# Matmuls whose moving tile and output are walked in short runs from several segments

## Chip, cores and metric

The kernel runs on one core of a Trainium2 chip. The metric is the time of one execution on the device, in microseconds (us). Two timed executions of the kernel before took 899.40 and 896.99 us, a median of 898.19. A further execution was recorded by the hardware profiler; all profile lines come from it.

## The reference

One block of an encoder: 512 tokens of width 1024. Three token mixers work on a normalised copy of the input, each has a gate, the gated sum goes through an output projection and is added to the input, and a feed-forward part with a short convolution follows.

```python
h = rms_norm(x, mix_norm_g[l])
proj = h @ w_in[l]                                  # q, k, v, o, gates of all mixers, merge_pre
...
gates = sigmoid(merge_pre + b_merge_gate[l])
g_ml, g_na, g_xa = split(gates, 3)
merged = g_ml * (y_ml @ w_br_ml[l]) + g_na * (y_na @ w_br_na[l]) + g_xa * (y_xa @ w_br_xa[l])
x = x + merged @ w_out[l]
a, u = split(rms_norm(x, ffn_norm_g[l]) @ w_up, 2)  # 2816 features each
x = x + (gelu(dwconv3(a, w_conv, b_conv)) * u) @ w_down
```

All of it is float32.

## The kernel before

Activations lie with features on the 128 partitions and tokens along the free dimension, so a projection gives one tile of 128 output features by 512 tokens at a time. A tile is one bank of the accumulation memory (PSUM), 512 float32 for each partition.

A float32 product is made out of three matmuls in a rounded float32 type (`F32R`): weights and activations are both split in a high and a low part, and `mm3` (L204) adds high times high (L205), high weight times low activation (L206) and low weight times high activation (L207) into the same output. The stationary operand is a block of 128 x 128 weights; the moving operand is 512 tokens of one block of 128 input features.

`proj` (L348) makes one tile: it takes the split weights of a block from `weights(key)`, a bank from a pool, and calls `mm3` for the 8 blocks of input features (`KT`, 1024 / 128), 24 matmuls in all. The keys name the projection: `mlk`, `xaq`, `o`, `memk`, `naq`, `nak` for the mixers' inputs, `g` for the merge gates (3 mixers by 8 tiles, L995), `out` for the output projection (8 tiles, L1039), and `ua` and `uu` for the two halves of the feed-forward up projection (22 tiles each, L1178 to L1203). Feature tile 0 of `ua` and `uu` is written out with `mm3` directly (L1176 to L1187), so 21 tiles of each go through `proj`. Tiles of the down projection (`dn`) and of the branches (`br`) call `mm3` without `proj`.

Weights come from memory in blocks by DMA from SyncE's queue, three blocks ahead, and are split by ScalarE (L187) and VectorE (L188) one block ahead. The order of the work is the order of the program: TensorE takes its matmuls one after another, and the mixers' smaller steps (generators that `step` advances) are put in between the projections. A result tile is read by VectorE or ScalarE as a whole: the gates at L996, the output at L1040, `ua` in `conv` at L391, `uu` at L1202.

In the neighbourhood attention, the scores (L747 and L748) take their moving tile as 8 rows of 32 columns, 64 columns apart, `KS[e][:, :, CW[b]:CW[b] + 32]`, and write 256 contiguous columns; the values (L785) take 256 contiguous columns. The transposes at L766 are plain float32 matmuls with 128 columns.

Of the kernel before, what the change touches and what calls it, by code (L numbers as in the profile page):

```python
# [20 lines left out]
KT = D // P  # L21
# [83 lines left out]
def hybrid_block(ctx, tc, xg, xT, memT, wflat, vecs, gbias, nabias, outa, outb):  # L105
# [27 lines left out]
    def mmps():  # L133
        return mmp.tile([P, 512], F32, tag="mm", name=nm("mm"))
# [58 lines left out]
    def weights(key):  # L193

        i, _, n = BINDEX[key]
        while st["raw"] <= min(i + RAW_AHEAD, len(BLOCKS) - 1):
            emit_raw(st["raw"])
            st["raw"] += 1
        while st["split"] <= min(i + SPLIT_AHEAD, len(BLOCKS) - 1):
            emit_split(st["split"])  # L200
            st["split"] += 1
        return split.pop(i)

    def mm3(ps, lh, ll, rh, rl, start, stop):  # L204
        PE.matmul(ps, lh, rh, start=start, stop=False)  # L205
        PE.matmul(ps, lh, rl, start=False, stop=False)  # L206
        st["mm"] = PE.matmul(ps, ll, rh, start=False, stop=stop).ins  # L207
# [137 lines left out]

    norm = []

    def proj(key, XHs, XLs, n=S, bank=None, at={}):  # L348
        ws = weights(key)
        ps = (bank or mmps)()  # L350
        for k in range(KT):
            mm3(ps[:, :n], ws[k][0], ws[k][1], XHs[k], XLs[k], k == 0, k == KT - 1)
            if k in at:
                at[k]()
        return ps
# [3 lines left out]
    for k in range(KT):  # L359
        if k % 2 == 0:  # L360
            ws = weights(("mlq", k // 2))
# [4 lines left out]
        for f in range(4):  # L366
            fs = slice(f * P, (f + 1) * P)
            if k == 0 and f == 0:
# [3 lines left out]
                for i, (w, x, j) in enumerate(((wh, XH, 0), (wl, XH, 0), (wh, XH, 1), (wl, XH, 1), (wh, XL, 0), (wh, XL, 1))):  # L372
                    PE.matmul(ps_q[0][:, hs[j]], w[:, fs], x[0][:, hs[j]], start=i == 0, stop=False)
                continue
            mm3(ps_q[f], wh[:, fs], wl[:, fs], XH[k], XL[k], k == 0, k == KT - 1)

    ps_k = [proj(("mlk", 0), XH, XL, bank=atps, at={1: lambda: norm.append(rstd_cols(acc, S, "x")),
                                                    7: lambda: norm.append(rstd_row(norm[0], S, "x"))})]
    rc, rb = norm
    ps_k.append(proj(("mlk", 1), XH, XL, bank=atps))  # L380
    SY.dma_start(gbf, gbias.partition_broadcast(P))
    rcc = cp.tile([P, NT], F32, name="rcc")
# [4 lines left out]
    def conv(ps, rbt, w, b, i, n):  # L387

        pad = pads[npad[0] % 2]
        npad[0] += 1  # L390
        V.tensor_tensor(pad[:, 1:513], ps, rbt, op=ALU.mult)  # L391
        t1 = scr()
        A.activation(t1, pad[:, 0:512], AF.Identity, scale=vcol(w, i), bias=vcol(b, i))  # L393
        V.scalar_tensor_tensor(t1, pad[:, 1:513], vcol(w, n + i), t1, op0=ALU.mult, op1=ALU.add)  # L394
        V.scalar_tensor_tensor(t1, pad[:, 2:514], vcol(w, 2 * n + i), t1, op0=ALU.mult, op1=ALU.add)  # L395
        return t1
# [9 lines left out]
    for f in range(4):  # L406
        ps = ps_k[f] if f < 2 else proj(("mlk", f), XH, XL)
        silu2(kT, slice(f * S, (f + 1) * S), conv(ps, rb, "mlw", "mlb", 4 + f, 8))
# [26 lines left out]
    for c in range(4):  # L435
        n = 272 if c == 0 else 256
        pss = [(mmps if c % 2 else atps)() for _ in range(NT)]
        for h in range(2):
            ws = weights(("tm", c, h))
            for t in range(NT):  # L440
                tsl = slice(t * P, (t + 1) * P)
                for k in range(4):
                    kk = 4 * h + k
                    ps = pss[t][:, :n]
                    mm3(ps, XH[kk][:, tsl], XL[kk][:, tsl], ws[k][0], ws[k][1], kk == 0, kk == KT - 1)
        for t in range(NT):
            ps = pss[t]
# [479 lines left out]
    for f in range(4):  # L927
        ps = proj(("xaq", f), XH, XL)
# [3 lines left out]
    for f in range(4):  # L932
        ps = proj(("o", f), XH, XL)
# [15 lines left out]
    for f in range(4):  # L949
        ps = proj(("memk", f), MH, ML, M)  # L950
# [3 lines left out]
    for i in range(4):  # L954
        ws = weights(("memv", i))
# [10 lines left out]
    for f in range(4):  # L966
        ps = proj(("naq", f), XH, XL)
# [3 lines left out]
    for f in range(4):  # L971
        ps = proj(("nak", f), XH, XL)
# [12 lines left out]
    for br in range(3):  # L985
# [18 lines left out]
        for fp in range(4):  # L1004
# [5 lines left out]
            ws = weights(("br", br, fp))  # L1010
            for i in range(2):
                f = 2 * fp + i
                ps = mmps()
# [22 lines left out]
    for f in range(KT):  # L1036
        xr = scr()
        SY.dma_start(xr, xT[f])
        ps = proj(("out", f), GH, GL)  # L1039
# [130 lines left out]
    for hh in range(2):  # L1170
# [3 lines left out]
        for j in range(HF):  # L1174
            f = HF * hh + j
            if f == 0:  # L1176
# [7 lines left out]
                k = KT - 1  # L1184
# [8 lines left out]
            c = conv(pa, rb2, "ffw", "ffb", f, FT)  # L1193
# [10 lines left out]
        for f in range(KT if hh == 0 else LF - 1):  # L1204
            ws = weights(("dn", hh, f, 0)) + weights(("dn", hh, f, 1))
            ps = mmps()
# [123 lines left out]
```

## Time and profile before

| what | value |
|---|---|
| median of two timed runs | 898.19 us |
| profiled execution | 899.74 us |
| its span, first to last instruction | 898.0 us |
| mean granted TensorE clock | 1.000 |
| VectorE, ScalarE, GpSimd busy | 579.5, 451.6, 165.2 us |
| matmuls of 128 x 512 at L205, high weights from `wh`, tokens from a unit tile, into an `mm` bank | 1022, mean 397 ns |
| weight loads at L205 | 1076, mean 188 ns |
| DMA, mean over the span | 111 GB/s |

A matmul's duration runs from its start to a modelled end, and the next matmul begins before that; the distance from one start to the next tells what a matmul costs in a row of them. Group lines give line, engine, operation, output and inputs, shape, count, then busy time, mean duration in ns, and the idle time of the engine before them with what ended it. Lines of a timeline give start and length in us, then the same names.

### The profile page before, as it was taken

Reading aid. Unit: us, or ns where it says so; the run is one execution under the profiler, and the core shown is the slowest. Engines: PE = TensorE matmul, PEld = TensorE weight load, DVE = VectorE, ACT = ScalarE, POOL = GpSimd, SP = SyncE. Lnnn points to the kernel's source line nnn. Section 1 sums busy time; section 2 is a strip of 40 time slices with the busy share of each in tenths; the row PEclk is TensorE's granted clock in tenths of the full one; section 3 lists DMA queues with packets and bytes.
Section 4 is the critical chain, followed back from the end, with each engine's and each line's share of the span. In section 5 each row is a group of like instructions: output and inputs, shape, how many; then the busy total and the mean of one; then the engine's idle time right before and its main releaser. Section 6 shows DMA issues by size and latency. Waiting matters only on the chain.

```text
span 898.0 us, 12449 instructions
## 1 busy us (share of the span) xinstructions
PE 890.3 (99%) x4446; PEld 747.2 (83%) x4446; DVE 579.5 (65%) x1154; ACT 451.6 (50%) x950; POOL 165.2 (18%) x236
## 2 busy tenths in 40 slices
PE   9999999999999999999999999999999999999997
PEld 7899878988888888888888888888888888888887
DVE  6794586756566757998766547766733476667433
ACT  6463455645545647899634435444422344444442
POOL 4201231102070660420000211111100011111010
PEclk9999999999999999999999999999999999999999
DMA  7223643422242453443323422222132322222412
GB/s 250 95 91 127 191 143 105 165 95 94 84 128 71 118 141 106 140 131 118 118 94 106 141 105 93 96 95 93 65 100 95 116 95 94 94 94 88 132 39 94
DMA packets 39293, 99.69 MB, mean 111 GB/s; under 512 B 5688, under 2 KB 13624, under 8 KB 39232
## 3 DMA queue, kind: packets, MB, share of 16 engines
q1 hardware_dynamic: 31584, 92.39, 29.8%
q0 software_dynamic: 7360, 6.32, 3.1%
q8 instruction: 35, 0.57, 0.3%
q14 instruction: 26, 0.21, 0.1%
q10 hardware_dynamic: 288, 0.20, 0.1%
HBM read 94.67 MB, written 4.21 MB: 110 GB/s over the span
## 4 chain that ended last, share of the span: by engine, by line
PE 95%; DMA 1%; ACT 1%; DVE 1%; issue 1%; POOL 0%; SPq 0%; POOLq 0%; DVEq 0%
PE mm L206 28%; PE mm L205 28%; PE mm L207 28%; PE at L205 2%; PE at L206 2%; PE at L207 2%; PE at L785 1%; PE at L640 1%; PE at L766 1%; PE at L608 1%; PE at L642 1%; DMA R<-rd 1%; DMA wr<-wflat 0%; PE at L623 0%; PE at L873 0%
## 5 line engine op out<-in xcount | busy, mean ns | idle before, releaser
L205 PE MATMUL mm<-u,wh 128*128 128x512 f32 (+1 forms) x1076 | 420.6, 391 | 0.5 <-ACT wh L187 0.5
L206 PE MATMUL mm<-u,wh 128*128 128x512 f32 (+1 forms) x1076 | 418.8, 389 | 0.0
L207 PE MATMUL mm<-u,wl 128*128 128x512 f32 (+1 forms) x1076 | 417.4, 388 | 0.0
L187 ACT ACTIVATE wh<-wr 128x512 fp32r<-128x512 f32 (+1 forms) x298 | 185.2, 624 | 264.7 <-PE mm L206 219.3
L188 DVE TENSOR_TENSOR wl<-wr,wh 128x512 fp32r<-128x512 f32 (+3 forms) x299 | 212.6, 712 | 113.2 <-ACT wh L187 108.5
L205 PEld LDWEIGHTS mm<-u,wh 128*128 128x128 f32 x1076 | 202.6, 188 | 43.6 <-ACT wh L187 0.8
L207 PEld LDWEIGHTS mm<-u,wl 128*128 128x128 f32 x1076 | 202.6, 188 | 43.5
L206 PEld LDWEIGHTS mm<-u,wh 128*128 128x128 f32 x1076 | 202.7, 188 | 42.1 <-DVE u L212 0.3
L1199 POOL TENSOR_TENSOR s<-s,rb 128x512 f32<-128x512 f32 x22 | 36.9, 1676 | 258.2 <-DVE s L1198 250.1
L473 POOL DMA_DIRECT2D u<-nav_d x128 | 62.3, 516 | 75.2 <-PE at L785 34.5
L211 ACT ACTIVATE u<-s 128x512 fp32r<-128x512 f32 x26 | 16.4, 631 | 53.5 <-DVE s L1202 53.2
L1047 POOL TENSOR_TENSOR acc<-acc,s 128x512 f32<-128x512 f32 x7 | 9.1, 1302 | 128.2 <-ACT s L1046 128.2
L1202 DVE TENSOR_TENSOR s<-mm,s 128x512 f32<-128x512 f32 x22 | 15.2, 689 | 21.4 <-POOL s L1199 21.4
L393 ACT ACTIVATE s<-pad,vec 128x512 f32<-128x512 f32 x30 | 24.4, 813 | 8.6 <-DVE pad L391 8.6
L212 DVE SCALAR_TENSOR_TENSOR u<-s,u 128x512 fp32r<-128x512 f32 x26 | 18.0, 692 | 14.3 <-ACT u L211 14.1
L394 DVE SCALAR_TENSOR_TENSOR s<-pad,vec,s 128x512 f32<-128x512 f32 x30 | 22.5, 751 | 6.1 <-ACT s L393 6.1
L205 PE MATMUL mm<-wh,u 128*128 128x256 f32 (+1 forms) x80 | 24.6, 307 | 0.0
L206 PE MATMUL mm<-wl,u 128*128 128x256 f32 (+1 forms) x80 | 24.4, 304 | 0.0
L207 PE MATMUL mm<-wh,u 128*128 128x256 f32 (+1 forms) x80 | 24.3, 304 | 0.0
L1198 DVE SCALAR_TENSOR_TENSOR s<-s,s 128x512 f32<-128x512 f32 x22 | 15.2, 692 | 13.4 <-ACT s L1197 13.3
L395 DVE SCALAR_TENSOR_TENSOR s<-pad,vec,s 128x512 f32<-128x512 f32 x30 | 22.5, 751 | 0.8
L1197 ACT ACTIVATE s<-s 128x512 f32<-128x512 f32 x22 | 13.9, 632 | 15.6 <-DVE s L1196 15.5
(295 smaller groups left out, 1056.6 us busy)
## 6 DMA issues: line engine op xcount, KB each, us to landing
wr<-wflat SPq DMA_DIRECT2D x140, 512.0 KB, 3.3
nab<-nabias SPq DMA_DIRECT2D x16, 256.0 KB, 2.6
u<-nav_d POOLq DMA_DIRECT2D x128, 32.0 KB, 2.6
s<-xT SPq DMA_DIRECT2D x15, 256.0 KB, 4.0
wr<-wflat SPq DMA_DIRECT2D x15, 192.0 KB, 2.4
nav_d<-nv POOLq DMA_DIRECT2D x8, 256.0 KB, 3.4
R<-rd SPq DMA_DIRECT2D x8, 256.0 KB, 3.6
wr<-wflat SPq DMA_DIRECT2D x2, 544.0 KB, 3.2
```

The costliest lines, as they stand in the source:

```text
L187: A.activation(h[:, u:v], src, AF.Copy)
L188: V.tensor_tensor(l[:, u:v], src, h[:, u:v].bitcast(F32), op=ALU.subtract)
L205: PE.matmul(ps, lh, rh, start=start, stop=False)
L206: PE.matmul(ps, lh, rl, start=False, stop=False)
L207: st["mm"] = PE.matmul(ps, ll, rh, start=False, stop=stop).ins
L211: A.activation(h, src, AF.Copy, scale=scale)
L212: V.scalar_tensor_tensor(l, src, scale, h.bitcast(F32), op0=ALU.mult, op1=ALU.subtract)
L393: A.activation(t1, pad[:, 0:512], AF.Identity, scale=vcol(w, i), bias=vcol(b, i))
L394: V.scalar_tensor_tensor(t1, pad[:, 1:513], vcol(w, n + i), t1, op0=ALU.mult, op1=ALU.add)
L395: V.scalar_tensor_tensor(t1, pad[:, 2:514], vcol(w, 2 * n + i), t1, op0=ALU.mult, op1=ALU.add)
L473: G.dma_start(vw[r * 32:(r + 1) * 32, i * 256:(i + 1) * 256], nav_v[hf, r, CW[b]:CW[b] + 32, hp * 256:(hp + 1) * 256])
L1199: G.tensor_tensor(c, c, rb2, op=ALU.mult)
```

## The change

`proj` takes moving tile and output tile in another order of columns. For four keys the 512 columns are seen as `a` segments; a run of `c` columns is taken from each segment in turn, then the next run of each. The same order is used for the high and the low moving tile and for the output, so each column's sum still lands in its own place.

```diff
+    def turned(a, key):
+
+        seg = {"ua": (2, 16), "uu": (2, 2), "g": (8, 16), "out": (4, 32)}.get(key[0])
+        return a.rearrange("p (a b c) -> p b a c", a=seg[0], c=seg[1]) if seg else a
+
     def proj(key, XHs, XLs, n=S, bank=None, at={}):
         ws = weights(key)
         ps = (bank or mmps)()
         for k in range(KT):
-            mm3(ps[:, :n], ws[k][0], ws[k][1], XHs[k], XLs[k], k == 0, k == KT - 1)
+            mm3(turned(ps[:, :n], key), ws[k][0], ws[k][1], turned(XHs[k], key), turned(XLs[k], key), k == 0, k == KT - 1)
```

| key | segments | columns in a segment | run, columns | runs in 512 columns |
|---|---|---|---|---|
| `ua` | 2 | 256 | 16 | 32 |
| `uu` | 2 | 256 | 2 | 256 |
| `g` | 8 | 64 | 16 | 32 |
| `out` | 4 | 128 | 32 | 16 |

The other keys, the tiles that call `mm3` directly and all other engines' instructions stay as they are.

## The prediction

> **What bounds the kernel now.** I read the page from the top: busy shares first, then the slices, then the chain of waits, then the costliest groups.
>
> ```profile
> span 898.0 us, 12449 instructions
> ...
> PE 890.3 (99%) x4446; PEld 747.2 (83%) x4446; DVE 579.5 (65%) x1154; ACT 451.6 (50%) x950; POOL 165.2 (18%) x236
> ...
> PE   9999999999999999999999999999999999999997
> ...
> PEclk9999999999999999999999999999999999999999
> ...
> PE 95%; DMA 1%; ACT 1%; DVE 1%; issue 1%; POOL 0%; SPq 0%; POOLq 0%; DVEq 0%
> PE mm L206 28%; PE mm L205 28%; PE mm L207 28%; PE at L205 2%; PE at L206 2%; PE at L207 2%; PE at L785 1%; PE at L640 1%; PE at L766 1%; PE at L608 1%; PE at L642 1%; DMA R<-rd 1%; DMA wr<-wflat 0%; PE at L623 0%; PE at L873 0%
> ...
> L205 PE MATMUL mm<-u,wh 128*128 128x512 f32 (+1 forms) x1076 | 420.6, 391 | 0.5 <-ACT wh L187 0.5
> ```
>
> TensorE carries 95% of the chain, is busy in every slice at the full granted clock, and the groups that the change touches (lines 205 to 207) waited half a microsecond in all. No other engine is near its limit. So what one matmul of those groups costs more or less is paid or gained in full, once per matmul. That cost isn't the 391 ns of the group's mean: matmuls overlap, and what counts is the distance from one start to the next. The timeline of the up projections has it:
>
> ```profile
> 699.75 0.39 PE L205 MATMUL mm<-u,wh 128*128 128x512 f32 x1
> 699.98 0.39 PE L206 MATMUL mm<-u,wh 128*128 128x512 f32 x1
> 700.21 0.39 PE L207 MATMUL mm<-u,wl 128*128 128x512 f32 x1
> 700.44 0.40 PE L205 MATMUL mm<-u,wh 128*128 128x512 f32 x1
> ```
>
> (start, duration, both in us.) One start every 0.23 us; over all 3,075 pairs of neighbours with 512 columns and less than 260 ns between them the mean is 231 ns, and it is the same whether VectorE, ScalarE and GpSimd stand idle in that stretch (230.4) or VectorE and ScalarE are both busy (231.2). Matmuls with 256 contiguous columns start 118 ns apart. The difference, 113 ns for 256 columns, makes 0.44 ns a column and some 5 ns fixed: columns set the time, not contention and not the weight load (188 ns in its rows, inside the 231).
>
> **What the change does to the work.** Moving tile and output get the same permutation, so each output column still receives its own sums, at its own place; nothing downstream sees another layout. In the program's order every engine keeps its instructions in the same sequence, and only TensorE's waits on its own semaphore differ: nine matmuls gain such a wait and nine lose one. A stall of that sort is at most the longest gap I found among the 256-column groups, 306 ns against 118; nine times 0.19 us is 1.7 us either way, and as many go as come, so I take nothing.
>
> What remains is the access pattern of 1,776 matmuls with 512 columns, counted from the loops (8 k-steps by 3 products a tile):
> - gates: 24 tiles, 576 matmuls, 32 runs of 16 columns;
> - output: 8 tiles, 192 matmuls, 16 runs of 32;
> - `ua`: 21 tiles (feature tile 0 is written out by hand and stays), 504 matmuls, 32 runs of 16;
> - `uu`: 21 tiles, 504 matmuls, 256 runs of 2.
>
> **Price of a run change, from the nearest row.** One place of this kernel already reads its moving tile in runs: the scores of the neighbourhood attention (L747, L748) take 8 runs of 32 columns, 64 apart, into contiguous output; L785 in the same stage takes 256 contiguous columns.
>
> ```profile
> 347.02 0.28 PE L747 MATMUL at<-KS,QS 128*128 128x256 f32 x1
> 347.14 0.28 PE L748 MATMUL at<-KS,QZ 128*128 128x256 f32 x1
> 347.26 0.28 PE L747 MATMUL at<-KS,QS 128*128 128x256 f32 x1
> 347.38 0.28 PE L748 MATMUL at<-KS,QZ 128*128 128x256 f32 x1
> 347.50 0.64 PE L785 MATMUL at<-w,u 128*128 128x256 f32 x4
> 347.98 0.60 PE L766 MATMUL at<-ident,s 128*128 128x128 f32 x4
> ```
>
> Again about 120 ns from start to start. Averaged over the trace, with gaps over 150 ns left out, runs of 32 take 120.4 ns (63 gaps), L785 takes 119.4 (57), and all of the other 256-column matmuls take 118.1 (620). Against its own stage that is 1.0 ns for 7 run changes, 0.14 ns each; against the rest 2.3 ns, 0.33 each; the worst gaps that recur (132 ns) would make 2 ns each; and the commonest (117 to 119) make none. Runs of 16 and 32 are near this row, so I take 0.14: 31 changes cost 4.3 ns, times 1,080 matmuls of gates and `ua` is 4.7 us; 15 changes cost 2.1 ns, times 192 of the output is 0.4 us.
>
> Runs of 2 are far from it: the reader of the moving tile and the writer of the sums both jump after every second column, 8 bytes, and come back later for the neighbours. No row here shows that. The low end is the same 0.14 ns, 36 ns a matmul, or nothing; the high end by the worst recurring gaps is 255 times 2, 510 ns. Between them lies a rate that this TensorE does show: the plain float32 transposes (L766) come every 109 ns for 128 columns, 0.85 ns a column, half the rate of the matmuls in question. I take that: with two columns of each run useful before the next jump, I expect the array to be fed at half rate. 512 columns at 0.85 ns are 436 ns, 205 more than 231, times 504 is 103.3 us.
>
> A rule of the Trainium skill bears on this place (Advanced Engine Details and Errata, section Memory Cachelines): two hits in a line of 16 bytes are enough to hide the memory's latency, and in PSUM, with lines of 8 bytes, every two consecutive elements should be contiguous. Runs of two float32 just fulfil both; by that `uu` would cost nothing, and the sum would be only the small terms. The trace has no runs this short, so it can't say yet whether the rule holds.
>
> **Sum.** 103.3 + 4.7 + 0.4 = 108 us. Nothing hides it, since TensorE is the chain, and nothing else grows: the other engines only get more time per tile. The profiled execution took 899.7 us (898.0 of span and 1.7 around it); it becomes 1,008. The median of the two timed runs is 898.2, 1.5 lower, so I forecast **1,006 us**, with 950 to 1,030 as this case's own range, since a bubble at each pair need not be a whole column long.
>
> **Rivals.**
> *Free runs (898 us).* If two neighbouring columns are all that reader and writer take at once, a jump after every pair breaks nothing. For it speaks that the commonest gaps of the 32-column runs equal contiguous ones; against it, that those runs are sixteen times as long and their output is contiguous. With 0.14 ns per change on gates, `ua` and output alone it is 903 us, so 893 to 903. This is the case that the skill's rule above leads to. Chance 0.20.
>
> *A small price per jump (952 us).* 0.33 ns at each change: 84 ns on each `uu` matmul (42.4 us), 10.2 on gates and `ua` (11.0 us), 5 on the output (1.0 us), 54 us together. By 0.14 it is 23 us, 922. For it speaks that it only extends measured rows; against it, that a price so far under a column's 0.44 ns is an average over jumps that mostly cost nothing. Chance 0.17.
>
> *All four groups are hurt (about 1,260 us).* If it is the scattered output that costs, with the run's length of no account, all 1,776 lose 205 ns: 364 us. The worst recurring gap, 2 ns per change, gives nearly the same: 257 + 67 + 6 = 330 us, 1,228. The attention rows say nothing of a scattered output, but their 8 runs speak against 2 ns as a general price. Chance 0.10. The same section of the Trainium skill also says that any non-contiguous pattern in PSUM slows matmuls significantly, which leads here; no run so far shows it.
>
> *Faster (875 us).* The 231 ns may hold some idle: the plain float32 transposes take 128 columns in 109 ns, and exactly twice that rate would take 512 columns in 218. If the other 13 ns come from walking one stretch of memory in order, and turns between segments spread the accesses, all 1,776 gain 13 ns: 23 us. It decides from 10 ns a matmul (18 us over 1,776). The runs of 32 in the attention show none of it: no mean below the contiguous one. Chance 0.08.
>
> **Numbers.** About 2%, 18 us, is what a measurement of this kernel tells from no change. Half-rate `uu` 0.45, small price 0.17, all hurt 0.10: slower 0.72. Free runs 0.20: within 2%. Faster 0.08. The range leaves out the faster case and the all-hurt one (0.18) and runs from 893, the low side of free runs, to 1,040, the forecast with 1 ns per change on gates, `ua` and output, half of the worst recurring price (36 us).
>
> **What will show it.** Start-to-start times by group in the timeline: `uu` alone at some 436 ns and the three others at 231 to 236 would bear the forecast out; 231 everywhere, the free case; 315 on `uu`, the small price; `ua`, gates and output also near 430, the scattered output; about 218 everywhere, the faster case. The page should keep TensorE at 99% in each case. A grown idle column before lines 205 to 207, or a chain that leaves TensorE, would show that what I priced at nothing, the waits, mattered. My forecast is wrong above all if the step from runs of 32 to runs of 2 is as flat as the commonest gaps suggest, or if the writer of the sums, of which this trace shows only contiguous output, has its own price.

## The result, and the profile after

Two timed runs of the changed kernel took 956.45 and 957.32 us, a median of 956.88 against 898.19: 58.7 us slower, a ratio of 1.0658 with a 95% interval of 1.0638 to 1.0678. The profiled execution's span grew from 898.0 to 955.6 us, 57.6.

The page of the changed kernel, its busy row, its slices of TensorE and of the granted clock, its chain and the first group of the change:

```profile
span 955.6 us, 12443 instructions
...
PE 947.9 (99%) x4446; PEld 751.5 (79%) x4446; DVE 574.7 (60%) x1154; ACT 453.0 (47%) x950; POOL 157.9 (17%) x236
...
PE   9999999999999999999999999999999999999997
...
PEclk9999999999999999999999999999999999999999
...
PE 96%; ACT 1%; DMA 1%; issue 1%; POOL 0%; DVE 0%; SPq 0%; POOLq 0%; ACTq 0%; DVEq 0%
...
L205 PE MATMUL mm<-u,wh 128*128 128x512 f32 (+1 forms) x1076 | 440.6, 410 | 1.0 <-ACT wh L187 1.0
```

The bound didn't move: TensorE is still 99% busy, at the same clock, with as many matmuls, and still hardly waits. Its 57.6 us of extra busy time are the whole loss, so the matmuls themselves must have become longer. The timeline shows where a tile of `ua` ends and one of `uu` begins (start and length in us; the differences of the first column are what counts):

```profile
596.39 0.40 PE L205 MATMUL mm<-u,wh 128*128 128x512 f32 x1
596.63 0.41 PE L206 MATMUL mm<-u,wh 128*128 128x512 f32 x1
596.88 0.41 PE L207 MATMUL mm<-u,wl 128*128 128x512 f32 x1
597.12 0.49 PE L205 MATMUL mm<-u,wh 128*128 128x512 f32 x1
597.45 0.52 PE L206 MATMUL mm<-u,wh 128*128 128x512 f32 x1
597.79 0.50 PE L207 MATMUL mm<-u,wl 128*128 128x512 f32 x1
598.13 0.50 PE L205 MATMUL mm<-u,wh 128*128 128x512 f32 x1
```

`ua` starts a matmul every 0.24 us, `uu` every 0.33 us, where both had 0.23. A tile of `uu` in the kernel before:

```profile
539.72 0.39 PE L205 MATMUL mm<-u,wh 128*128 128x512 f32 x1
539.95 0.39 PE L206 MATMUL mm<-u,wh 128*128 128x512 f32 x1
540.17 0.40 PE L207 MATMUL mm<-u,wl 128*128 128x512 f32 x1
```

The trace records the access pattern of each matmul's moving tile, so the groups can be averaged apart (start to start, neighbours with the same pattern; gaps that hold another wait, some 40 ns or more above the group's median, are left out here and below):

| group | runs | ns, before 231.0 | more, times matmuls |
|---|---|---|---|
| `uu` | 256 of 2 | 329.9 | 98.9 x 504 = 49.8 us |
| `ua` | 32 of 16 | 241.6 | 10.6 x 504 = 5.3 us |
| gates | 32 of 16 | 237.5 | 6.5 x 576 = 3.7 us |
| output | 16 of 32 | 235.6 | 4.6 x 192 = 0.9 us |

The sum, 59.7 us, agrees with the loss of 58.7 us to 1 us. Divided by the run changes, these are 0.39, 0.34, 0.21 and 0.31 ns: it looks as though each change of run had a price of a third of a nanosecond. The experiments ask whether it has.

### The profile page after: what moved, and what is told of

It reads as the page before. It is cut to its first block, busy times and chain, and to the rows that moved or that the text cites. A ratio compares the mean times of both kernels' runs of the same rounds, so it can differ in the third digit from the quotient of the medians.

```text
span 955.6 us, 12443 instructions
## 1 busy us (share of the span) xinstructions
PE 947.9 (99%) x4446; PEld 751.5 (79%) x4446; DVE 574.7 (60%) x1154; ACT 453.0 (47%) x950; POOL 157.9 (17%) x236
## 4 chain that ended last, share of the span: by engine, by line
PE 96%; ACT 1%; DMA 1%; issue 1%; POOL 0%; DVE 0%; SPq 0%; POOLq 0%; ACTq 0%; DVEq 0%
PE mm L206 29%; PE mm L207 29%; PE mm L205 28%; PE at L205 2%; PE at L206 2%; PE at L207 2%; PE at L790 1%; PE at L645 1%; PE at L771 1%; PE at L613 1%; PE at L647 1%; DMA wr<-wflat 0%; PE at L628 0%; PE at L878 0%; PE at L752 0%
## 5 line engine op out<-in xcount | busy, mean ns | idle before, releaser
L205 PE MATMUL mm<-u,wh 128*128 128x512 f32 (+1 forms) x1076 | 440.6, 410 | 1.0 <-ACT wh L187 1.0
L206 PE MATMUL mm<-u,wh 128*128 128x512 f32 (+1 forms) x1076 | 439.7, 409 | 0.0
L207 PE MATMUL mm<-u,wl 128*128 128x512 f32 (+1 forms) x1076 | 439.0, 408 | 0.0
L188 DVE TENSOR_TENSOR wl<-wr,wh 128x512 fp32r<-128x512 f32 (+3 forms) x299 | 207.6, 696 | 169.2 <-ACT wh L187 166.7
L205 PEld LDWEIGHTS mm<-u,wh 128*128 128x128 f32 x1076 | 204.3, 190 | 61.9 <-issue 3.4
L1204 POOL TENSOR_TENSOR s<-s,rb 128x512 f32<-128x512 f32 x22 | 28.6, 1302 | 320.3 <-DVE s L1203 310.5
L396 DVE TENSOR_TENSOR pad<-mm,rb 128x512 f32<-128x512 f32 x22 | 15.1, 692 | 32.9 <-PE mm L207 32.9
L205 PE MATMUL mm<-wh,u 128*128 128x256 f32 (+1 forms) x80 | 24.5, 307 | 0.0
```

The source lines that it names most:

```text
L188: V.tensor_tensor(l[:, u:v], src, h[:, u:v].bitcast(F32), op=ALU.subtract)
L1204: G.tensor_tensor(c, c, rb2, op=ALU.mult)
```

## The experiments

### Which side pays: the reader of the moving tile or the writer of the sums

Two kernels that each keep one half of the change:

```diff
-            mm3(turned(ps[:, :n], key), ws[k][0], ws[k][1], turned(XHs[k], key), turned(XLs[k], key), k == 0, k == KT - 1)
+            mm3(ps[:, :n], ws[k][0], ws[k][1], turned(XHs[k], key), turned(XLs[k], key), k == 0, k == KT - 1)     # moving_only
+            mm3(turned(ps[:, :n], key), ws[k][0], ws[k][1], XHs[k], XLs[k], k == 0, k == KT - 1)                  # output_only
```

> Only the moving tile is walked in runs; the output is written in order, so the sums of these four projections stand at other tokens' places. The profile of the changed kernel has start-to-start times of 330 ns for runs of 2 (uu), 241 for runs of 16 (ua, gates), 236 for runs of 32 (out), 232 for contiguous tiles: 0.2 to 0.4 ns for each change of run. Theory 1, the reader of the moving tile pays: all of it stays, uu 330, ua and gates 241, about 957 us. Theory 2, the writer of the sums pays: uu and the others 231 to 232, about 898 us. Theory 3, each side pays a part and they add: between, e.g. uu 280 and 928 us. Theory 4, each alone is enough: 957 us here and also with the output alone.

> Only the output is written in runs; the moving tile is read in order, so the sums of these four projections stand at other tokens' places. Theory 1 (the reader pays): all tiles at 231 to 232 ns, about 898 us. Theory 2 (the writer pays): uu 330, ua and gates 241, 957 us. Theory 3 (parts that add): what moving_only leaves of the 59 us. Theory 4 (either is enough): 957 us.

With the moving tile alone: 959.21 us, ratio 1.0678 (1.0657 to 1.0699) to the kernel before, and `uu` at 329.9 ns, `ua` at 241.6, as in the changed kernel. With the output alone: 897.85 us, ratio 1.0002 (0.9992 to 1.0011), all matmuls with 512 columns together at the mean of the kernel before. Told apart by their place in the program's order, those of `uu` take 230.9 ns, as before. A tile of `uu` in the second kernel:

```profile
548.93 0.40 PE L205 MATMUL mm<-u,wh 128*128 128x512 f32 x1
549.16 0.40 PE L206 MATMUL mm<-u,wh 128*128 128x512 f32 x1
549.40 0.39 PE L207 MATMUL mm<-u,wl 128*128 128x512 f32 x1
```

The old 0.23 us a start. Theory 1 holds: the reader pays everything. So that two segments don't merely hide a price of the writer, one more kernel writes runs of 2 from many more segments, again with the moving tile in order:

```diff
-        seg = {"ua": (2, 16), "uu": (2, 2), "g": (8, 16), "out": (4, 32)}.get(key[0])
+        seg = {"ua": (16, 2), "uu": (128, 2), "g": (8, 2), "out": (4, 2)}.get(key[0])
...
+            mm3(turned(ps[:, :n], key), ws[k][0], ws[k][1], XHs[k], XLs[k], k == 0, k == KT - 1)
```

> Only the output is written in runs, all of 2 columns, from 8 (gates), 16 (ua), 128 (uu) and 4 (out) segments: the patterns that cost the reader 437 to 493 ns a matmul. The moving tile is read in order, so the sums stand at other tokens' places. If the writer of the sums has no price at all for runs of 2: 231 to 232 ns and 898 us. If it has one that 2 segments (output_only) merely hid: above 232, e.g. at the half rate 436 ns on 1,776 matmuls, 1,260 us.

897.63 us, ratio 0.9994 (0.9982 to 1.0007), and the group of L205 keeps its mean of 390 ns:

```profile
span 895.9 us, 12443 instructions
...
L205 PE MATMUL mm<-u,wh 128*128 128x512 f32 (+1 forms) x1076 | 419.7, 390 | 0.3 <-ACT wh L187 0.3
```

Scattering the sums in pairs costs nothing that this measurement can see.

### Is `uu` alone responsible

```diff
-        seg = {"ua": (2, 16), "uu": (2, 2), "g": (8, 16), "out": (4, 32)}.get(key[0])
+        seg = {"ua": (2, 16), "g": (8, 16), "out": (4, 32)}.get(key[0])
```

> uu is taken in order again, ua, gates and output stay as in the changed kernel. If each change of run has its price whatever else the kernel does: uu back to 231 ns (504 x 98 ns = 49 us less), the others stay at 241, 241 and 236, in sum 504 x 9.6 + 576 x 8 + 192 x 3.4 ns = 10 us above the kernel before: 908 us. If the small rises of ua and gates came only from the slower uu beside them, they fall too and the time is 898 us; if the threshold of my forecast were right (only runs of 2 cost), also 898 us.

908.08 us, ratio 1.0117 (1.0102 to 1.0132), and 241.2 ns still for `ua`. The parts add up: `uu` is worth the 49 us, the three others 10.

### Is it a price for each change of run

Other run lengths, first from few segments, then from many:

```diff
-        seg = {"ua": (2, 16), "uu": (2, 2), "g": (8, 16), "out": (4, 32)}.get(key[0])
+        seg = {"ua": (2, 4), "uu": (2, 8), "g": (8, 4), "out": (4, 2)}.get(key[0])       # shorter_runs
+        seg = {"ua": (16, 2), "uu": (128, 2), "g": (8, 2), "out": (32, 2)}.get(key[0])   # pairs_many_places
+        seg = {"ua": (16, 4), "uu": (4, 4), "g": (64, 4), "out": (2, 32)}.get(key[0])    # fours_many_places
```

> Other run lengths, otherwise as the changed kernel: ua runs of 4 (127 changes), uu runs of 8 (63), gates runs of 4 (127), out runs of 2 (255). Price by the change, 0.385 ns: ua and gates 231 + 49 = 280 ns, uu 255, out 330; 504 x 73 + 576 x 49 + 192 x 98 ns = 84 us, 982 us. Price by the run of 2 alone (a run too short for its piece of memory): ua, gates and uu near 241, out 330, about 933 us.

980.32 us, ratio 1.0921 (1.0899 to 1.0943): the sum that the price by the change gave (982), and yet its parts are wrong. Three places of its timeline, first output tiles (pairs from 4 segments), then gates (runs of 4 from 8 segments), then a tile of `ua` (runs of 4 from 2 segments):

```profile
524.46 0.62 PE L205 MATMUL mm<-u,wh 128*128 128x512 f32 x1
524.90 0.62 PE L206 MATMUL mm<-u,wh 128*128 128x512 f32 x1
525.35 0.62 PE L207 MATMUL mm<-u,wl 128*128 128x512 f32 x1
```

```profile
287.25 0.45 PE L206 MATMUL mm<-u,wh 128*128 128x512 f32 x1
287.53 0.45 PE L207 MATMUL mm<-u,wl 128*128 128x512 f32 x1
287.81 0.44 PE L205 MATMUL mm<-u,wh 128*128 128x512 f32 x1
```

```profile
624.22 0.42 PE L205 MATMUL mm<-u,wh 128*128 128x512 f32 x1
624.47 0.42 PE L206 MATMUL mm<-u,wh 128*128 128x512 f32 x1
624.72 0.42 PE L207 MATMUL mm<-u,wl 128*128 128x512 f32 x1
```

The pairs from 4 segments come every 0.44 us (mean 444.4 ns), where the price by the change had said 330; runs of 4 from two segments every 0.25 us (251.5), where it had said 280. The gates' 277.6 ns are near its 280, and `uu` takes 243.2 where it had said 255. The errors cancelled in the sum: that the total came out was luck. A kernel's time alone would have confirmed a wrong theory here; the groups' own distances refute it.

> Runs of 2 in all four groups, in both tiles, from other numbers of segments: gates 8 (64 columns apart), ua 16 (32 apart), out 32 (16 apart), uu 128 (4 apart). So far runs of 2 took 330 ns from 2 segments and 444 from 4; contiguous 232. Theory 1, a fixed price for each change of run, 0.385 ns: 330 in all four, 1,776 x 98 ns = 174 us, 1,072 us. Theory 2, what counts is how many places are visited in turn before a run's neighbours are read, with two places still partly held and more not at all: 444 in all four, 1,776 x 212 ns = 377 us, 1,275 us. Theory 3, the distance of the jump counts (256 columns cheaper than 128): the four differ by their distances, with uu (4 apart, all but in order) near 232.

1,311.01 us, a single run. All pairs are now near twice the contiguous 231 ns, whatever the distance: 436.8 (32 segments), 452.9 (128), 455.4 (16), and 491.9 for the gates (8). Theory 1 and the theory of the distance fall: even the pairs of `uu` that go forward 4 columns at a time, all but in order, take the double. Theory 2's ceiling of 444 is a little low.

> Runs of 4 from more segments: uu 4 (128 columns apart), ua 16 (32 apart), gates 64 (8 apart); out has runs of 32 from 2 segments (256 apart). So far runs of 4 took 251 ns from 2 segments and 280 from 8, runs of 32 took 235.6 from 4. Theory 1, the number of changes: uu, ua and gates alike (265 to 280), about 898 + 504 x 2 x 40 + 576 x 40 ns = 960 us or a little more. Theory 2, number of places with a ceiling: uu between 251 and 280, ua and gates 280 as with 8; out 235: 898 + 504 x 49 + 504 x 40 + 576 x 49 ns = 971 us. Theory 3, distance: uu (128) differs from ua (32) and gates (8), which come down towards 232.

924.64 us, a single run: `uu` (4 segments, 128 apart) 267.8 ns, `ua` (16, 32 apart) 243.2, gates (64, 8 apart) 232.1, output 236.4. Runs of 4 from 64 segments, 127 changes, cost 1 ns: only the theory of the distance had expected that of `ua` and gates, and for pairs it had just failed. A run of 4 is a different thing from a run of 2.

### What is special about four columns

Four float32 columns are 16 bytes. The guess is that the reader takes aligned pieces of that size, and that the moving tiles begin on the edge of one (their addresses are not in the trace). So the next kernels read from two places with explicit steps, and shift the start by 2 columns, so that each run begins and ends in the middle of an aligned piece of four:

```diff
+    def turned(a, key):
+
+        seg = {"ua": (2, 0, 16), "uu": (4, 2, 248), "g": (2, 0, 128), "out": (4, 0, 248)}.get(key[0])
+        if not seg:
+            return a
+        c, start, d = seg
+        return bass.AP(a.tensor, a.offset + start, [list(a.ap[0]), [c, S // 2 // c], [d, 2], [1, c]])
```

Here `c` is the run's length, `start` the first column and `d` the distance between the two places, in columns; only the moving tile goes through `turned`, and part of it is left out or read twice. The two kernels that follow it have, in the same order, `(4, 0, 64), (4, 0, 128), (16, 2, 240), (4, 0, 32)` and `(8, 2, 240), (256, 2, 240), (32, 2, 224), (16, 0, 240)`.

> Only the moving tile is walked in runs, always from two places d columns apart, whatever else of the tile is left out or read twice (so these sums are of other tokens); the output is in order. Runs of 2 with d = 16 (ua) and d = 128 (gates); runs of 4 with d = 248 from column 0 (out) and from column 2 (uu), where each run reaches over a boundary of 4 columns. If the number of places sets the price: ua and gates 330 ns as with d = 256. If the distance does: gates at 444, as out was with 4 segments 128 apart, and ua elsewhere. If a run's price is its change alone: uu and out alike, near 251. If the memory hands out aligned pieces of 4 columns and a half-used piece has to be fetched again: out near 251 and uu near 330 or above. With 330 for the pairs: 898 + 1,080 x 98 + 192 x 20 + 504 x 20 ns = 1,018 us without the pieces, with them (98 in place of the last 20) 1,057.

1,052.77 us, a single run, where the sum with the pieces had said 1,057 and without them 1,018. Runs of 4 from column 0 take 242.7 ns, the same runs from column 2 take 329.0; pairs take 329.5 with d = 128 and 327.5 with d = 16. The output tiles, then the feed-forward part, in which both pairs and shifted runs of 4 keep this distance:

```profile
544.29 0.41 PE L207 MATMUL mm<-u,wl 128*128 128x512 f32 x1
544.54 0.41 PE L205 MATMUL mm<-u,wh 128*128 128x512 f32 x1
544.78 0.41 PE L206 MATMUL mm<-u,wh 128*128 128x512 f32 x1
...
613.67 0.50 PE L205 MATMUL mm<-u,wh 128*128 128x512 f32 x1
614.01 0.50 PE L206 MATMUL mm<-u,wh 128*128 128x512 f32 x1
614.33 0.50 PE L207 MATMUL mm<-u,wl 128*128 128x512 f32 x1
```

The same number of run changes, the same length of run: the place of the boundaries differs, by 8 bytes, and 86 ns hang on it. The two groups read different tiles, but the next kernel reads runs of 4 from column 0 in the tiles of `uu` too, for about 251 ns. So a run's price isn't its change, and the aligned piece of 4 columns is what the numbers point to.

> Only the moving tile is walked in runs, from two places d columns apart, with part of the tile left out or read twice (so these sums are of other tokens). Runs of 4 with d = 64 (ua), 128 (uu), 32 (out); runs of 16 from column 2 with d = 240 (gates), so that each run begins and ends in the middle of an aligned piece of 4 columns. Whole pieces: if the distance of the jump sets the price, ua 280 ns as with 8 segments 64 apart, uu 268 as with 4 segments 128 apart, out 243 as with 16 segments 32 apart; if the number of places does, all three at 243 to 251 as with two segments. Gates: 241 if only the change of run counts; if split pieces are fetched again, 32 runs split 32 pieces at the price that pairs from two places pay, (330 - 241) / 128 = 0.7 ns for each extra visit, 22 ns more, 263.

951.26 us, a single run. Whole runs of 4 from two places: 242.6 ns (d = 32) and 251.3 for the two others together; neither reaches the 278 and 268 that 8 and 4 segments took at these distances (the 280 of the expectations still holds gaps with another wait), so the distance alone doesn't set the small price of whole pieces. Runs of 16 from column 2: 288.0, more than the 263 that I expected and 46 above the same runs from column 0. That suggested counting all visits: 32 runs of five pieces are 160 visits, and 160 times 1.8 ns (231 / 128, a contiguous tile's time for each of its pieces) is 288. The last kernel was to test that count.

> Only the moving tile is walked in runs, from two places, starting at column 2 (part of the tile left out or read twice, so these sums are of other tokens). Theory: each visit to an aligned piece of 4 columns costs 1.8 ns (231 / 128), unless the piece was used just before the last one. Runs of 8 from column 2 (ua, d = 240) touch 3 pieces each, 64 x 3 = 192 visits, 346 ns; runs of 32 from column 2 (gates, d = 224) 9 pieces each, 16 x 9 = 144 visits, 259 ns; two runs of 256 from column 2 (uu) 130 visits, 234 ns; aligned runs of 16 (out, d = 240) 128 visits, 231 to 242. Sum 504 x 114 + 504 x 2 + 576 x 27 + 192 x 9 ns = 76 us, about 975 us. Rival, a price for each change of run as in the changed kernel (0.385 ns): 63 changes 256, 15 changes 238, 1 change 232, 31 changes 241; 917 us.

981.16 us, a single run, 6 us above the count's forecast and 64 above the rival's. `ua` 348.7 ns (346 expected), gates 264.5 (259), `uu` 235.9 (234), aligned runs of 16 242.2. A piece of its timeline with `ua`:

```profile
611.26 0.53 PE L206 MATMUL mm<-u,wh 128*128 128x512 f32 x1
611.61 0.52 PE L207 MATMUL mm<-u,wl 128*128 128x512 f32 x1
611.96 0.52 PE L205 MATMUL mm<-u,wh 128*128 128x512 f32 x1
```

0.35 us a matmul, for 192 visits. `uu` begins at column 2 as well, but has one change of run, and takes 235.9 ns: it isn't the shifted start that costs, but the pieces that are split. All cells together:

| runs, start | places | visits to pieces of 4 | 1.8 ns each | measured, ns |
|---|---|---|---|---|
| contiguous | 1 | 128 | 231 | 231.0 |
| 256, column 2 | 2 | 130 | 234 | 235.9 |
| 32, column 2 | 2 | 144 | 260 | 264.5 |
| 16, column 2 | 2 | 160 | 288 | 288.0 |
| 8, column 2 | 2 | 192 | 346 | 348.7 |
| 2, column 0 | 4 | 256 | 461 | 444.4 |
| 2, column 0 | 8, 16, 32, 128 | 256 | 461 | 491.9, 455.4, 436.8, 452.9 |
| 2, column 0 | 2 | 256 | 461 | 330 |
| 4, column 2 | 2 | 256 | 461 | 329.0 |
| 4 to 32, column 0 | 2 to 64 | 128 | 231 | 232 to 278 |

Two things stay outside the count. Pairs, and shifted fours, from two places cost 330 instead of 461: as if the second visit to a piece were cheaper, (330 - 231) / 128 = 0.8 ns, when only one or two other pieces came between (here), and not with three or more (all the other split rows). No row speaks against that reading, but it was not tested by itself; and the pairs from 4 to 128 places scatter around the count, from 437 to 492 ns, for reasons that stay open. And whole pieces cost 1 to 47 ns more by an order that I can't reduce to the number of places or to their distance; 8 places 64 columns apart are the worst. What makes that price is open.

## Why the prediction was right and where it was wrong

The direction, the bound and the range were right; the likeliest case, 1,006 us, was not. That 956.9 us lies in the range says little, since 893 to 1,040 holds every case but two, from no change upwards. Point by point:

- **TensorE is the bound and hides nothing**: right. The extra busy time equals the extra span, 57.6 us.
- **Waits on its own semaphore, taken as nothing**: nothing contradicts it. Writing the output alone in runs leaves the time at 1.0002.
- **Runs of 16 and 32**, priced by the attention's runs of 32 at 0.14 ns a change, 4.7 + 0.4 us: right in kind, half in size. 5.3 + 3.7 + 0.9 = 9.9 us in the trace, 908.08 us for the kernel with these groups alone.
- **Runs of 2, at half rate, 436 ns, 103.3 us**: this is the term that failed, with 329.9 ns and 49.8 us. The idea behind it, that two columns before the next jump feed the array at half rate, holds for pairs from 4 or more places (437 to 492; `shorter_runs`, `pairs_many_places`). What I hadn't asked was how soon the other half of a piece is needed. With only two segments the very next visit but one comes back to it, and about half of the price is saved. That the early return is the reason is the reading above, which no run tested by itself; that two segments cost 330 ns, and four or more 437 and above, is measured. I also gave a part of it to the writer of the sums, which pays nothing.
- **The rival with a small price for each jump, 952 us**, came nearest to the time, 956.9, and for the wrong reason. The measured prices for a change run from 0.01 (runs of 4 from 64 segments) to 1.0 ns (pairs from 8), and to 1.8 and more for the runs of 8 to 32 from column 2; runs of 4 from two places cost 12 or 98 ns a matmul by their start. It was an average that fitted this mixture of runs.
- **Free runs**: refuted by `uu`. The rule of the Trainium skill on which it leaned (Advanced Engine Details and Errata, Memory Cachelines) names 16 bytes as the line of SBUF, and the shifted runs agree with that size, 242.7 against 329.0 ns; but two hits in such a line weren't enough here for full speed: 330 ns and more. Whole lines, four hits a visit, took 232 to 278 ns.
- **All four groups hurt by the scattered output**: refuted, 0.9994 (0.9982 to 1.0007) with pairs in all four. What the same section of the Trainium skill says of non-contiguous patterns in PSUM is not seen in any of these outputs, whose runs are of 2 columns or more.
- **Faster**: nothing of it; no order came below the contiguous 231 ns.
- **A reading and a sum**: the lines from 699.75 us that stand for the up projections are of the down projection, which the change doesn't touch. The distance is the same, 230.9 ns for `uu`, so nothing hangs on it. And 0.14 ns at every change makes 921 us, not 922.

## What to carry to other kernels

Count how often a matmul's moving tile enters an aligned group of 16 bytes: in these float32 tiles a visit took about 1.8 ns, less where the piece had been left only one or two visits before. So runs should begin and end on a multiple of four columns, and then their order costs less (1 to 47 ns of 231 here). The output tile was permuted in pairs at no cost that these runs can see, so a permutation that is wanted anyway can be put on the side of the sums. And where a change mixes several sizes, take the groups apart by their start-to-start times: for `shorter_runs` a wrong theory gave the right total (982 against 980), and only the groups showed it.

## What the runs showed of the hardware that was not expected

- For the reader of the moving tile, how a run lies on groups of four columns can matter more than its length: runs of 4 from 64 places took 232.1 ns, about as contiguous ones, and runs of 16 shifted by 8 bytes 288.0.
- The writer of the sums has no price for runs of 2 columns from 2 to 128 segments (ratios 1.0002 and 0.9994).
- Pairs from two places took 330 ns, from 4 to 128 places 437 to 492. By the reading above, not tested by itself, a half-used piece that is visited again after one or two others costs less than half of a full visit (0.8 against 1.8 ns).
- None of the orders tried on the moving tile was faster than the contiguous 231 ns.
